# A ring of 24 weight places instead of 22, each on a 1 KB boundary, paid for with the descriptor scratch

## The chip, the core and the metric

The kernel runs on one core of a Trainium2 chip. The metric is the device time of one execution in microseconds. Before the change the median of three runs is 1161.49 us (1161.32 to 1161.6). Engine names are those of the profile: PE is the matrix engine, DVE the vector engine, ACT the scalar engine, POOL the GpSimd engine, SP the engine that here issues nearly all loads; PEld is PE's weight load.

## What is computed

One layer of an encoder on a sequence of 256 tokens of width 1024, all in float32: a mixer (the "trunk" below), a layer norm, a mixture of 32 experts of which each token uses 4, and a second layer norm. Cut to the part that takes most of the time:

```
x  = layer_norm(alpha * x + mix(x))             # attention, pooling and an S5 branch, gated
logits = x @ w_router + b_router                 # 32 experts, the 4 largest per token
hu  = x_e @ w_up[e] + b_up[e]                    # 1024 -> 2048, for the tokens of expert e
act = x_glu * sigmoid(1.702 * x_glu) * (x_lin + 1)   # both clamped at 7
y_e = act @ w_down[e] + b_down[e]                # 1024 -> 1024
x  = layer_norm(alpha * x + sum_e gate_e * y_e)
```

The weights of one expert are 12 MB (2048 x 1024 and 1024 x 1024 numbers of 4 bytes), those of all 32 are 384 MB. Every weight is read from HBM once.

## The kernel before

**The ring.** All large weights come in chunks of 1 MB: 128 partitions of 8 KB. The trunk has 29 chunks (`N_TRUNK`), the experts 384: the experts are worked off in 16 pairs, and a pair has 24 chunks, 16 for `w_up` and 8 for `w_down`, the two experts in turn. The chunks live in a ring of `NW` places of 8 KB per partition (`place`, L82). `load_more` (L105) issues a load on SP's queue whenever a place is free, in the order of use; `done` (L122) gives a place back when the last product that reads its chunk has been written into the program, and so triggers the next load. The load itself then waits, in SP's queue, until PE has really read the place. Only the last two chunks differ: they are loaded together, in quarters with rows of 2 KB (L112 to L117).

**Places that hold something else.** At the start (L160) 12 places are taken from the ring for the trunk's own tiles (the input split in two halves, tables, work tiles); 10 are left for chunks. The trunk's tiles give their places back at fixed points (L702 to L710, L742 to L745), others ask for one (`keep`, L195, which takes the next place to come free). Near the end, in the last pair (L1144 to L1147), five places are taken for `row`, `base`, `z2` and two `lns`: the last loads have been issued by then.

**One pair.** Each token row of an expert sits in one of 64 slots. `up_chunk` (L1033) adds the bias and runs 16 chunk products for a quarter of the up projection; PE handles the two experts of a pair side by side, in two halves of its columns. `swiglu` runs on DVE and ACT between the matmuls. `gather` (L958) makes the next pair's inputs. `down_chunk` (L1041) runs the down projection, and `scatter` adds the gated result to four accumulators that stay in PSUM over all 16 pairs. In the last pair `residual` (DVE) and `add_residual` (PE) add the residual, and after the last scatter the second layer norm runs on all engines and the result goes out in four stores.

**The small loads.** `down_bias` (L1051), after pair 8, loads the 128 KB of `b_down` on POOL's queue into the tile that held the gated activations, and multiplies it with the gates in the next pair. `row_loads` (L1067), emitted in the last pair after `up_chunk(15, 1)`, loads the four rows of the layer norms' gains and offsets (4 KB each) on POOL's queue into one place of the ring, and POOL spreads each over all partitions (L1071). ACT's next instruction in the program after that point is the tanh of `swiglu` for `hu` of (15, 0).

**Completion counters.** A load signals its landing through one of eight counters that the program builder hands out in turn to all loads on SP's and ACT's queues together; a load waits until the one before it on the same counter has landed. Loads on POOL's queue have counters of their own.

**The place in memory.** Of each partition's memory, the first 16384 bytes are the descriptor scratch for POOL's loads, then come 128 bytes of constants, then the tiles of the pool `con` (L127 to L145, 3904 bytes with each tile rounded up to 32), then the ring. So the ring starts at 20416, which is 64 bytes below a multiple of 1 KB, and since a place is 8 KB every place does.

Of the kernel before, what the change touches and what calls it, by code (L numbers as in the profile page):

```python
# [7 lines left out]
F32 = mybir.dt.float32  # L8
# [10 lines left out]
NE = 32  # L19
NP = NE // 2  # L20
SLOT = 64
NW = 22
WARM = 8
ALPHA = 2.0 ** 0.25
EPS = 1e-5
# [38 lines left out]
def hybrid_layer(ctx: ExitStack, tc: tile.TileContext, wt, wm, pa, pb, pc, xin, bu, lnp, b_down, out):  # L64
    nc = tc.nc
    pe, act, dve, pool, sp = nc.tensor, nc.scalar, nc.vector, nc.gpsimd, nc.sync
    TT, TS, STT = dve.tensor_tensor, dve.tensor_scalar, dve.scalar_tensor_tensor

    con = ctx.enter_context(tc.tile_pool(name="con", bufs=1))
# [8 lines left out]
    state = {"next": 0}  # L78
    free = list(range(NW))
    wants = []  # L80
# [61 lines left out]
    ones32 = con.tile([128, 32], F32)  # L142
    epst = con.tile([128, 2], F32)
    hpi = con.tile([128, 1], F32)
    junk = con.tile([128, 1], F32)  # L145


    ph1 = ExitStack()
# [866 lines left out]
    def scatter(gT, y, n, first=False):  # L1015
        for t in range(2):
            pe.matmul(accs[t][n], gT[:, t * 128:(t + 1) * 128], y, start=first, stop=True, skip_group_check=True)  # L1017
# [32 lines left out]

    def down_bias():  # L1051
        bdn = mw.tile([32, D], F32, tag="at", name="bdn")
        pool.dma_start(out=bdn, in_=b_down)
        gTall = mw.tile([32, S], F32, tag="s0", name="gTall")
        pt = ph.tile([32, S], F32, tag="g", name="ptg")
        for t in range(2):
            pe.transpose(pt[:, t * 128:(t + 1) * 128], gate[:, t], ident)
        act.activation(out=gTall, in_=pt, func=ACTF.Copy)
        for n in range(2):
            pending.append(lambda n=n: scatter(gTall, bdn[:, n * 512:(n + 1) * 512], n))  # L1060
# [5 lines left out]

    def row_loads():  # L1067
        for i in range(4):
            pool.dma_start(out=row[32 * i:32 * i + 1, 0], in_=lnp[0, i:i + 1])
        for i in range(4):  # L1070
            pool.partition_broadcast(lns[i // 2][:, i % 2], row[32 * i:32 * i + 1, 0])  # L1071

# [65 lines left out]
    for p in range(NP):  # L1138
# [3 lines left out]
        for n in range(4):  # L1142
            hu = up_chunk(p, n, xg)
            if (p, n) == (NP - 1, 1):  # L1144

                row, base, z2, *lns = (place(free.pop(0)).rearrange("p (t d) -> p t d", t=2) for _ in range(5))
                row_loads()  # L1147
            if prev is not None:
                swiglu(*prev)
            if n == 2:  # L1150
                gT = gates_T(oh, gate[:, :, 2 * p:2 * p + 2])
            if n == 3 and p + 1 < NP:
                oh = hot(val[:, :, ahead])
            prev = (hu, at, n)
# [17 lines left out]
        if p + 1 == NP:  # L1172
            scatter(gT, y, 1)
        else:
            pending.append(lambda gT=gT, y=y, p=p: scatter(gT, y, 1, p == 0))
            if p == NP // 2:
                down_bias()
            xg = nxt
# [165 lines left out]
```

## Time and profile before

| | |
|---|---|
| median of 3 runs | 1161.49 us |
| profiled execution, its own time | 1161.53 us |
| span of the profiled execution | 1159.8 us |
| PE busy | 1130.4 us (97%) |
| PEld busy | 527.4 us (45%) |
| DVE, ACT, POOL busy | 300.9, 184.7, 13.5 us |
| moved by DMA | 438.05 MB, mean 378 GB/s |
| mean granted clock of TensorE | 0.997 |

The profile's page gives the busy time of each engine, then the span in 40 equal slices with the engines' busy tenths, the share of the 16 DMA engines' time that was used and the GB/s moved, then the groups of instructions and the loads. An engine's busy time is read against what the other engines did in the same stretch: ends of matmuls are modelled, so a PE that is shown busy is not thereby a PE at its peak. Waits are listed as "engine, line, what it waited for: total, times, longest".

### The profile page before, as it was taken

The numbers are of one execution on the slowest core, as the hardware profiler recorded it, in microseconds if no ns is written. First come the engines' busy times: TensorE is split into PE (matmuls) and PEld (weight loads), VectorE is DVE, ScalarE is ACT, GpSimd is POOL, SyncE is SP. The second block draws the span as 40 slices with busy tenths as digits, with TensorE's granted clock in tenths as the row PEclk, the third lists the DMA queues.
The fourth block names the chain that finished last, engine by engine and source line by source line (L and its number), as shares of the span: only waits on it lengthen the run. The fifth ranks groups of instructions, "written<-read, shape, count | busy, mean of one in ns | idle before, by whom it ended". The sixth has DMA issues, their size and how long they took to land. (4 is left out here: it accounts for less than half of the span.)

```text
span 1159.8 us, 13362 instructions
## 1 busy us (share of the span) xinstructions
PE 1130.4 (97%) x5535; PEld 527.4 (45%) x5535; DVE 300.9 (26%) x710; ACT 184.7 (16%) x389; POOL 13.5 (1%) x19
## 2 busy tenths in 40 slices
PE   9999999999999999999999999999999999999996
PEld 6888986643434343434343433343434344334332
DVE  4798622430202111111212121111111111111042
ACT  4555410310101010101010101010101010101002
POOL 0000000000000000000000000000000000000100
PEclk9999999999999999999999999999999999999999
DMA  9733685699999999999999999999999999999992
GB/s 368 306 110 137 243 358 212 253 423 421 420 421 421 421 421 421 421 421 420 421 422 420 421 421 420 414 422 420 422 421 420 422 420 421 421 421 420 420 412 87
DMA packets 63169, 438.05 MB, mean 378 GB/s; under 512 B 7136, under 2 KB 7648, under 8 KB 10752
## 3 DMA queue, kind: packets, MB, share of 16 engines
q1 hardware_dynamic: 62064, 435.46, 91.2%
q10 hardware_dynamic: 864, 1.54, 0.4%
q8 instruction: 45, 0.74, 0.3%
q0 software_dynamic: 176, 0.15, 0.0%
q14 instruction: 20, 0.16, 0.0%
HBM read 436.07 MB, written 1.05 MB: 377 GB/s over the span
## 5 line engine op out<-in xcount | busy, mean ns | idle before, releaser
L1028 PE MATMUL hu<-w,xg 128*64 128x512 f32 x2048 | 480.9, 596 | 14.2 <-DMA w<-in_wm_dram 14.2
L1028 PEld LDWEIGHTS hu<-w,xg 128*64 128x64 f32 x2048 | 166.0, 137 | 316.0 <-issue 262.1
L1028 PE MATMUL py<-w,at 128*64 128x512 f32 x1024 | 231.5, 597 | 0.0
L1000 DVE TENSOR_SCALAR s<-hu 128x256 f32<-128x256 f32 x64 | 27.0, 422 | 581.6 <-PE hu L1028 581.6
L1028 PEld LDWEIGHTS py<-w,at 128*64 128x64 f32 x1024 | 70.5, 136 | 136.0 <-issue 129.6
L1011 ACT ACTIVATE at<-pta 128x256 f32<-128x256 f32 x64 | 24.5, 383 | 422.9 <-PE pta L1010 422.9
L1037 PE MATMUL hu<-bup,pc_sb 128*64 128x512 f32 x256 | 68.3, 605 | 0.0
L1017 PE MATMUL acc<-y,gT 128*128 128x512 f32 x128 | 63.5, 618 | 1.5 <-ACT y L1045 1.5
L248 PE MATMUL pm<-w,w 128*128 128x256 f32 x208 | 60.6, 291 | 0.8 <-ACT vsb L641 0.8
L965 PE MATMUL pg<-oh,x 128*128 128x128 f32 x512 | 59.9, 275 | 0.0
L249 PE MATMUL pm<-w,w 128*128 128x256 f32 x208 | 58.8, 283 | 0.0
L250 PE MATMUL pm<-w,w 128*128 128x256 f32 x208 | 58.8, 282 | 0.0
L965 PEld LDWEIGHTS pg<-oh,x 128*128 128x128 f32 x512 | 58.4, 192 | 0.1
L1001 ACT ACTIVATE hu<-s 128x256 f32<-128x256 f32 x64 | 24.6, 385 | 168.3 <-DVE s L1000 168.3
L1045 ACT ACTIVATE y<-py 128x512 f32<-128x512 f32 x32 | 19.1, 597 | 190.9 <-PE py L1028 190.9
L234 DVE TENSOR_TENSOR w<-w,w 128x1024 fp32r<-128x1024 f32 x30 | 36.5, 1219 | 19.3 <-ACT w L233 19.1
L248 PEld LDWEIGHTS pm<-w,w 128*128 128x128 f32 x208 | 39.7, 191 | 3.8 <-issue 1.7
L1017 PEld LDWEIGHTS acc<-y,gT 128*128 128x128 f32 x128 | 21.7, 189 | 42.9 <-issue 39.7
L249 PEld LDWEIGHTS pm<-w,w 128*128 128x128 f32 x208 | 39.8, 191 | 0.1
L250 PEld LDWEIGHTS pm<-w,w 128*128 128x128 f32 x208 | 39.8, 191 | 0.0
L233 ACT ACTIVATE w<-w 128x1024 fp32r<-128x1024 f32 x30 | 31.6, 1057 | 35.3 <-PE pm L250 25.1
L408 PE MATMUL pm<-w,w 128*128 128x256 f32 x160 | 36.1, 383 | 1.1 <-DMA w<-in_wt_dram 1.1
(320 smaller groups left out, 681.8 us busy)
## 6 DMA issues: line engine op xcount, KB each, us to landing
w<-in_wm_dram SPq DMA_DIRECT2D x382, 1024.0 KB, 19.8
w<-in_wt_dram SPq DMA_DIRECT2D x26, 1024.0 KB, 7.9
w<-in_wm_dram SPq DMA_DIRECT2D x8, 256.0 KB, 11.7
w<-in_wt_dram SPq DMA_DIRECT2D x4, 256.0 KB, 5.6
w<-in_wt_dram ACTq DMA_DIRECT2D x4, 256.0 KB, 5.9
w<-in_wt_dram SPq DMA_DIRECT2D x2, 512.0 KB, 5.0
w<-in_xin_dram SPq DMA_DIRECT2D x1, 1024.0 KB, 7.7
w<-in_pb_dram SPq DMA_DIRECT2D x1, 896.0 KB, 8.5
```

The lines of the kernel that those rows point to most:

```text
L233: act.activation(out=hi, in_=src, func=ACTF.Copy)
L234: TT(lo, src, hi.bitcast(F32), op=ALU.subtract)
L248: pe.matmul(out, whi, ahi, start=first, stop=False)
L249: pe.matmul(out, whi, alo, start=False, stop=False)
L250: pe.matmul(out, wlo, ahi, start=False, stop=last)
L408: pe.matmul(dst, w[:, k * 128:(k + 1) * 128], xt3[:, k], start=(k == 0), stop=(k == 7))
L965: pe.matmul(pg[:, b], x1[:, t, k * 128:(k + 1) * 128], oh[:, t], start=(t == 0), stop=(t == 1))
L1000: TS(xg, hu[:, 0:256], 7.0, None, op0=ALU.min)
L1001: act.activation(out=th, in_=xg, func=ACTF.Tanh, scale=0.851)
L1017: pe.matmul(accs[t][n], gT[:, t * 128:(t + 1) * 128], y, start=first, stop=True, skip_group_check=True)
L1028: pe.matmul(dst[64 * e:64 * e + 64], lhs[:, k, 64 * e:64 * e + 64], w[:, k % 4], start=first and k == 0, stop=(k == 7))
L1037: pe.matmul(hu[64 * e:64 * e + 64], ident[:, i:i + 1].to_broadcast([128, 64]), bup, start=True, stop=False)
```

## The change

`NW` goes from 22 to 24. The descriptor scratch shrinks from 16 KB to 1 KB. The tile `junk` becomes a column of a tile `scr` of 96 bytes. The ring then starts at 1024 + 128 + 3872 + 96 = 5120 bytes, a multiple of 1 KB, and so does every place. The trunk still takes 12 places, from the end of a longer list; 12 are left for its chunks instead of 10. The load of `b_down` and the four row loads move from POOL's queue to ACT's; the spreading of the rows stays on POOL.

```diff
-NW = 22
+NW = 24
...
-    junk = con.tile([128, 1], F32)
+
+    scr = con.tile([128, 24], F32)
+    junk = scr[:, 0:1]
...
         bdn = mw.tile([32, D], F32, tag="at", name="bdn")
-        pool.dma_start(out=bdn, in_=b_down)
+        act.dma_start(out=bdn, in_=b_down)
...
         for i in range(4):
-            pool.dma_start(out=row[32 * i:32 * i + 1, 0], in_=lnp[0, i:i + 1])
+            act.dma_start(out=row[32 * i:32 * i + 1, 0], in_=lnp[0, i:i + 1])
...
-    nc = _bacc.Bacc("TRN2", target_bir_lowering=False, num_devices=1)
+    nc = _bacc.Bacc("TRN2", target_bir_lowering=False, num_devices=1, dynamic_dma_scratch_size=1024)
```

## Rows read from the trace of the kernel before

**Rows 1.** The page, span in 40 slices: DMA busy tenths, GB/s.
```profile
DMA  9733685699999999999999999999999999999992
GB/s 368 306 110 137 243 358 212 253 423 421 420 421 421 421 421 421 421 421 420 421 422 420 421 421 420 414 422 420 422 421 420 422 420 421 421 421 420 420 412 87
```
**Rows 2.** Windows: engines' busy us (instructions), PEclk, DMA share, GB/s.
```profile
180.00:200.00 20.00, 20.00 (x73) 13.52 (x72) 6.82 (x16) 0.00 (x0) 0.00 (x0) 1.00 0.52 204
200.00:220.00 20.00, 19.67 (x159) 13.56 (x158) 10.91 (x39) 7.58 (x14) 1.54 (x2) 1.00 0.75 286
220.00:231.00 11.00, 11.00 (x67) 5.74 (x67) 2.63 (x10) 1.83 (x4) 0.00 (x0) 1.00 0.32 117
231.00:240.00 9.00, 9.00 (x44) 2.98 (x42) 2.13 (x6) 1.05 (x3) 0.00 (x0) 1.00 1.01 422
240.00:1125.00 885.00, 870.38 (x3972) 334.99 (x3968) 148.19 (x360) 90.02 (x215) 7.70 (x9) 1.00 1.01 421
```
**Rows 3.** Waits of SP's queue: two of 177 to 231 us, one of 240 to 1125.
```profile
SPq L109 <- PE mix L789: 25.1, 3, 9.9
SPq L109 <- PE hu L1028: 10.1, 1, 10.1
...
SPq L109 <- DMA w<-in_wm_dram: 662.0, 318, 3.6
```
**Rows 4.** Waits of PE: one of 0 to 230 us, two of 340 to 1150.
```profile
PE pm L408 <- DMA w<-in_wt_dram: 1.1, 4, 0.6
...
PE hu L1028 <- DMA w<-in_wm_dram: 14.2, 24, 1.3
PE acc L1017 <- DMA bdn<-in_b_down_dram: 0.4, 1, 0.4
```
**Rows 5.** Timeline of PE: first bias product of pairs 2, 7, 9, 15.
```profile
330.46 1.03 PE L1037 MATMUL hu<-bup,pc_sb 128*64 128x512 f32 x4
...
603.63 1.03 PE L1037 MATMUL hu<-bup,pc_sb 128*64 128x512 f32 x4
...
721.27 1.08 PE L1037 MATMUL hu<-bup,pc_sb 128*64 128x512 f32 x4
...
1081.09 1.03 PE L1037 MATMUL hu<-bup,pc_sb 128*64 128x512 f32 x4
```
**Rows 6.** Timeline of the end: start, us, instruction [idle before <- what ended it].
```profile
1116.92 3.65 PE L1028 MATMUL hu<-w,xg 128*64 128x512 f32 x14 [0.41 <-DMA w<-in_wm_dram]
...
1121.90 0.20 PEld L1028 LDWEIGHTS py<-w,at 128*64 128x64 f32 x4 [0.84 <-DMA w<-in_wm_dram]
...
1126.26 1.98 PE L1083 MATMUL acc<-w,pc_sb 128*128 128x512 f32 x4 [0.34 <-DVE w L1078]
1129.38 1.98 PE L1083 MATMUL acc<-w,pc_sb 128*128 128x512 f32 x4 [1.14 <-DVE w L1078]
...
1155.82 0.36 ACTq L1210 DMA_DIRECT2D out_dram<-w  x1
```
**Rows 7.** The page, DMA issues: KB each, median us from issue to landing.
```profile
w<-in_wm_dram SPq DMA_DIRECT2D x382, 1024.0 KB, 19.8
```
**Rows 8.** One window among the loads in quarters, rows of 2 KB.
```profile
1128.00:1129.00 1.00, 0.24 (x1) 0.00 (x0) 0.96 (x2) 0.00 (x0) 0.00 (x0) 1.00 1.00 393
```
**Rows 9.** Timeline of POOL, ACT, PE: the small loads and what stands beside them.
```profile
721.72 0.83 POOL L1053 DMA_DIRECT2D bdn<-in_b_down_dram  x1 [505.58 <-DMA w<-in_wm_dram]
...
1091.50 1.93 POOL L1069 DMA_DIRECT2D w<-in_lnp_dram  x4 [368.95 <-PE hu L1028]
1099.39 4.94 POOL L1071 PARTITION_BROADCAST w<-w  x4 [5.97 <-DMA w<-in_wm_dram]
...
1091.73 0.39 ACT L1001 ACTIVATE hu<-s 128x256 f32<-128x256 f32 x1 [9.74 <-DVE s L1000]
...
1100.76 0.44 PE L1010 MATMUL pta<-pc_sb,s 128*128 128x128 f32 x2
...
0.73 1.86 ACTq L170 DMA_DIRECT2D w<-in_wt_dram  x4
```

## The prediction, made before the change was run

> **What bounds the kernel now.** I read the slices of the page first, then windows cut where the slices change, then the waits of SP and PE, last the timeline at the end. PE is shown busy for 97% of the span, and that row would mislead. The slices show two regimes of the DMA engines [rows 1]: in the first 230 us they are at nine tenths only at the start and idle for long stretches after it, and from the ninth slice on they stand at nine tenths and 420 to 423 GB/s up to the last but one. The windows give the edge: full from 231 us on (share 1.01), and 421 GB/s from 240 to 1125 us [rows 2].
>
> Whether PE waits for these loads is seen from the distance between pairs. From pair 2 to pair 7 a pair takes (603.63 - 330.46) / 5 = 54.63 us, from pair 9 to pair 15 (1081.09 - 721.27) / 6 = 59.97 us [rows 5]. The work of a pair is the same. 24 chunks of 1.0486 MB at 421 GB/s take 59.8 us. So the later pairs run at the pace of the loads, and the earlier ones at PE's own, 9% faster, off the stock that the ring had gathered in the trunk. PE's listed idle time for loads, 14.2 us in 24 waits [rows 4], is only the part that the modelled ends leave. The last waits for a load are at 1116.92 and 1121.90 us [rows 6]; what follows waits for DVE (1126.26, 1129.38) and runs down to the last store at 1155.82 without a load in its way.
>
> What held the loads back before 231 us is in SP's queue: between 177 and 231 us it waited for PE to finish reading places, 25.1 us in three waits on the trunk's last products and 10.1 us on the first expert's [rows 3]. The ring was full and the DMA engines had nothing to do. From 240 us on SP waits 662.0 us for earlier landings: there are eight in flight (19.8 us from issue to landing [rows 7], one landing every 2.49 us).
>
> **The change, part by part.** *Two more places.* They are free at the start, when the list of places is handed out: two more trunk chunks are loaded at once, and from then on each release triggers the load two chunks further on than before. When PE starts on the experts, two more chunks are in. Room for them: between 180 and 231 us the DMA engines are idle for 20 x 0.48 + 20 x 0.25 + 11 x 0.68 = 22.1 us [rows 2], and more before [rows 1]; two chunks need 2 x 1.0486 MB / 421 GB/s = 4.98 us. From 231 us on the stream is unbroken either way, so every landing comes 4.98 us earlier, that for which PE waits at 1121.90 too. PE starts the experts at the same time and has 9% of speed in hand; with 5.0 us more stock, and 59.97 - 54.63 = 5.34 us of it used up in a pair, it begins to wait about one pair later and still waits in the last pairs. The tail behind 1121.90 keeps its length. Term: -4.98 us. The bounds: no more than this from two places, and 0 if the advance is lost (below).
>
> *The trunk.* The two extra loads stand behind the loads that are needed first, and take about 5.0 us of DMA time in the first 50 us, where it is busy. PE waited for trunk chunks 1.1 us in 230 us [rows 4], and no chunk is issued later than before in the order of use. I take 0; the upper end is 5.0 us, if PE had to wait that long, which would be passed on in full, since the loads of the experts wait for PE there.
>
> *Places on a boundary.* The trace has no row of a load into a place that starts on one, so this is bounded by what each row costs apart from its bytes. With the share at 1.00, rows of 2 KB move at 393 GB/s [rows 8], rows of 8 KB at 421 [rows 2]. Per DMA engine that is 83.4 ns and 311.3 ns a row, so 227.9 ns for 6144 bytes, and about 7.4 ns that do not depend on the size, 2.4% of an 8 KB row. If the start 64 bytes below the boundary were all of it, the stream of 883 us from 239 to 1122 us would lose 21 us. The other end lies below nothing by as much as the slowest full slice, 414 GB/s against 421 [rows 1], 1.7% or 15 us. I take 0, by the row nearest to it: 421 GB/s in every slice with rows that all start off the boundary, and a fixed part that any row would have.
>
> [...]
>
> *The small loads on ACT.* `bdn` takes POOL 0.83 us at 721.72, PE waited 0.4 us for it [rows 4, 9]. On ACT it stands behind the copy of `y` and ahead of the copy of the gates, and waits for the same products as that `y`; its issue costs some 0.47 us by ACT's own four loads at the start (1.86 us [rows 9]). PE runs at the pace of the loads there and makes it up in the next pair: 0, between -0.4 and +0.5 us. The four row loads took POOL 1.93 us at 1091.50, as soon as the place was read [rows 9]. On ACT they are 1.86 us ahead of the tanh of (15, 0), queued behind them with everything that ACT does for that pair. ACT sat idle for 9.74 us before that tanh; with 24 places `row` gets one that PE has read half an up projection earlier, so the issue falls into this gap. And even when late, the transposes that need the tanh start at 1100.76, 9 us on. POOL spreads the rows at 1099.39 for 4.94 us, and their first reader, `residual`, comes after 1120. Term: 0; without the cover 1.86 us.
>
> *The smaller scratch* holds descriptors of loads on POOL's queue, of which none are left: 0.
>
> The sum is made on the profiled execution: 1161.53 - 4.98 = 1156.55 us. That execution is 0.04 us over the median of the runs, so 1156.5 us. The four zeros may move it by 1 us: 1155.5 to 1157.5.
>
> **The rivals.** *Loads into aligned places are faster.* For it: the fixed 7.4 ns a row [rows 2, 8]. Against it: nothing says that this is the offset. PE has the speed to follow (54.63 against 59.97 us a pair). In full 1156.5 - 21 = 1135.5 us; with half, 1146.
>
> *The advance is lost:* the extra loads make the trunk late by as much as they gain, or the stock is not there at 231 us. For it: the DMA engines are full in the first slice. Against it: 1.1 us of waits in the trunk, 22.1 us of idle DMA before 231. Time 1161.5 us.
>
> *ACT's queue becomes the wait, slower than before.* The moved loads now share the eight counters with SP's stream, and a row load may have to wait for a landing of the stream, with the tanh of (15, 0) behind it. Each turn of waiting costs 2.49 us; four in a row, 10 us, still lie in the gap and the cover above. From 18 us on (9.74 + 9) PE stands, and from 18 + 5 = 23 us the kernel is slower than before. If the rows were handed counters of the last loads, ACT would stand until 1137 - 5 = 1132 us; the transposes would start at about 1134 and not at 1095.8, and the time would be some 1195 us. Against it: POOL's rows were issued at once, between loads of the stream; nothing in the program puts them behind the last ones.
>
> *Aligned places are slower* by the 1.7% above: 1171 us.
>
> **How the numbers follow.** Forecast 0.76; faster loads 0.10; advance lost 0.07; ACT's wait 0.05; slower loads 0.02. 0.2% is 2.3 us, about what a measurement of this kernel can tell from no change. Faster by more than that: 0.76 + 0.10 = 0.86; within it 0.07; slower 0.05 + 0.02 = 0.07. The range goes from 1147 (the smaller half of the faster loads) to 1159 us: it holds 0.76 and about 0.05 of the rivals. The forecast's own range is 1155.5 to 1157.5.
>
> **What would show it.** In the profile after, full DMA from the same 231 us at the same 421 GB/s; pairs of PE 54.6 us apart up to pair 7 and 59.9 from pair 9 or 10 on, pair 15 starting near 1076; the last wait for a load at about 1117. A rate above 425 GB/s is the first rival; PE waits for loads in the first 230 us the second; an idle stretch of PE in the last pair ended by ACT the third. I am wrong on the main step if the last pairs do not wait for loads, or if pair 15 starts where it did.

## The result: 17.6 us less, and only 5 of them from the two places

The changed kernel takes 1143.99 us (median of 4 runs, 1143.88 to 1144.09), the kernel before on the same chip 1161.55 us (4 runs, 1161.32 to 1162.25). The ratio is 0.9848, with a 95% interval from 0.9831 to 0.9865. The forecast was 1156.5 us; the time lies 12.5 us below it, between the two prices that the first rival gave for faster loads (1146 and 1135.5). The profiled execution has a span of 1142.0 us and a time of its own of 1143.99 us. Of the ten executions of e4 below one took 4417.05 us; it is left out of the ratio there.

### The profile after

The slices of the page, as [rows 1]: DMA busy tenths, GB/s moved.

```profile
DMA  9923596599999999999999999999999999999992
GB/s 370 388 96 133 236 360 250 221 415 427 427 427 426 426 426 426 426 427 427 427 427 426 427 426 426 421 427 426 427 427 426 428 426 427 426 426 426 412 425 97
```

The DMA engines are still full from the ninth slice on, and they still have idle time before it. Two things are new. The second slice moves 388 GB/s instead of 306, some 2.2 MB more: the two extra chunks (e1, with 24 places, has 385 there, e2, with 22, has 308). And the rate: 426 or 427 GB/s in nearly every full slice, where [rows 1] had 420 to 422 in nearly all. The windows put this beside [rows 2] (engines' busy us with instructions in brackets, granted clock, DMA share, GB/s):

```profile
180.00:200.00 20.00, 20.00 (x74) 13.50 (x73) 6.84 (x16) 0.00 (x0) 0.00 (x0) 1.00 0.54 200
200.00:220.00 20.00, 19.67 (x161) 13.66 (x160) 10.92 (x39) 7.58 (x14) 1.54 (x2) 1.00 0.77 290
220.00:231.00 11.00, 11.00 (x66) 5.66 (x66) 2.63 (x10) 1.83 (x4) 0.00 (x0) 1.00 0.32 128
240.00:1100.00 860.00, 853.59 (x3942) 322.13 (x3940) 144.51 (x354) 89.43 (x213) 4.94 (x4) 1.00 1.01 426
```

From 180 to 231 us the kernel is nearly unchanged: the ring is full, and 0.46 x 20 + 0.23 x 20 + 0.68 x 11 = 21.3 us of DMA time stay idle (22.1 before). The stream then starts at the same moment, runs at the same share of 1.01 and carries 426 GB/s instead of 421. Nothing is faster by doing less: 382 loads of 1 MB stand on the page as in [rows 7], and each now lands 19.6 us after its issue, not 19.8:

```profile
w<-in_wm_dram SPq DMA_DIRECT2D x382, 1024.0 KB, 19.6
```

PE's timeline at the first bias product of pairs 2, 7, 9, 12 and 15, as [rows 5] (start, us of one, instruction):

```profile
330.25 1.03 PE L1039 MATMUL hu<-bup,pc_sb 128*64 128x512 f32 x4
...
603.42 1.03 PE L1039 MATMUL hu<-bup,pc_sb 128*64 128x512 f32 x4
...
713.11 1.08 PE L1039 MATMUL hu<-bup,pc_sb 128*64 128x512 f32 x4
...
886.72 1.03 PE L1039 MATMUL hu<-bup,pc_sb 128*64 128x512 f32 x4
...
1064.74 1.03 PE L1039 MATMUL hu<-bup,pc_sb 128*64 128x512 f32 x4
```

Pairs 2 to 7 are 54.63 us apart, as before: that is PE's own pace, and it has not moved. From pair 9 to 12 a pair takes (886.72 - 713.11) / 3 = 57.9 us, a mixture, and from 12 to 15 (1064.74 - 886.72) / 3 = 59.3 us, which is the pace of the loads again (24 x 1.0486 MB at 426 GB/s are 59.1 us). PE therefore starts to wait later, and the waits agree (engine, line, what it waited for: us in total, times, longest). Against [rows 4], 14.2 us in 24 waits, the same stretch of 340 to 1150 us now has

```profile
PE hu L1030 <- DMA w<-in_wm_dram: 6.3, 15, 1.2
```

and the trunk, where [rows 4] had 1.1 us in four waits, has one:

```profile
PE pm L410 <- DMA w<-in_wt_dram: 0.2, 1, 0.2
```

At the end, in place of [rows 6]:

```profile
1099.73 3.65 PE L1030 MATMUL hu<-w,xg 128*64 128x512 f32 x14 [0.28 <-DMA w<-in_wm_dram]
...
1104.69 0.20 PEld L1030 LDWEIGHTS py<-w,at 128*64 128x64 f32 x4 [0.83 <-DMA w<-in_wm_dram]
...
1109.06 1.98 PE L1085 MATMUL acc<-w,pc_sb 128*128 128x512 f32 x4 [0.35 <-DVE w L1080]
1112.18 1.98 PE L1085 MATMUL acc<-w,pc_sb 128*128 128x512 f32 x4 [1.14 <-DVE w L1080]
...
1138.27 0.40 ACTq L1212 DMA_DIRECT2D out_dram<-w  x1
```

The last two waits for a load end 17.19 and 17.21 us earlier than in [rows 6]. From the last of them to the last store the two kernels take 33.92 and 33.58 us. So all but 0.3 us of the gain is in when the loads land, and not in the tail. The place to look is the stream of loads between 231 and 1105 us.

### The profile page after: what moved, and what is told of

Its sections match the earlier page's. It is cut to its first block, busy times and chain, and to the rows that moved or that the text cites. A ratio compares the mean times of both kernels' runs of the same rounds, so it can differ in the third digit from the quotient of the medians.

```text
span 1142.0 us, 13355 instructions
## 1 busy us (share of the span) xinstructions
PE 1122.2 (98%) x5535; PEld 518.0 (45%) x5535; DVE 300.7 (26%) x710; ACT 184.8 (16%) x389; POOL 10.8 (1%) x14
## 5 line engine op out<-in xcount | busy, mean ns | idle before, releaser
L1030 PE MATMUL hu<-w,xg 128*64 128x512 f32 x2048 | 471.6, 596 | 6.4 <-DMA w<-in_wm_dram 6.3
L1030 PEld LDWEIGHTS hu<-w,xg 128*64 128x64 f32 x2048 | 155.7, 137 | 309.6 <-issue 278.7
L250 PE MATMUL pm<-w,w 128*128 128x256 f32 x208 | 60.6, 292 | 0.8 <-ACT vsb L643 0.8
L251 PE MATMUL pm<-w,w 128*128 128x256 f32 x208 | 58.8, 283 | 0.0
L252 PE MATMUL pm<-w,w 128*128 128x256 f32 x208 | 58.8, 283 | 0.0
L971 ACT ACTIVATE xg<-pg,pc_sb 128x128 f32<-128x128 f32 x64 | 29.3, 458 | 48.1 <-DVE xg L973 48.1
## 6 DMA issues: line engine op xcount, KB each, us to landing
w<-in_wm_dram SPq DMA_DIRECT2D x382, 1024.0 KB, 19.6
```

The costliest lines, as they stand in the source:

```text
L250: pe.matmul(out, whi, ahi, start=first, stop=False)
L251: pe.matmul(out, whi, alo, start=False, stop=False)
L252: pe.matmul(out, wlo, ahi, start=False, stop=last)
L971: act.activation(out=xg[:, k], in_=pg[:, b], func=ACTF.Identity, scale=l1[:, k:k + 1], bias=l1[:, 8 + k:9 + k])
L1030: pe.matmul(dst[64 * e:64 * e + 64], lhs[:, k, 64 * e:64 * e + 64], w[:, k % 4], start=first and k == 0, stop=(k == 7))
```

## The experiments

Theory after the result: the two places give the 5 us of the forecast, and the boundary gives the rest, through the rate. Rivals: the smaller scratch or the moved loads do it; or the alignment that counts is not that of the places, but of the source; or it needs 24 places to show. For reading the edits: the width of `scr` decides where the ring starts. With 24 floats it starts at 5120, and every 8 floats more or less move it, and with it every place and each tile behind the ring, by 32 bytes. All ratios are to the kernel before, run beside it.

### The four corners: places and boundary, each alone

**e1: all of the change, but places 64 bytes below a boundary of 1 KB** (192 past one of 256 bytes).

```diff
-    scr = con.tile([128, 24], F32)
+    scr = con.tile([128, 8], F32)
```

> The changed kernel with one thing undone: scr is 32 bytes instead of 96, so the ring of 24 starts 64 bytes below a 1 KB boundary, as before the change. Theory A (the boundary sped the loads up): the full windows fall from 426 to 421 GB/s, a chunk lands every 2.49 us instead of 2.46, and the time is 1144.0 + 11.4 = 1155.4 us (1154 to 1157). Theory B (the smaller scratch, the loads off POOL's queue or the 24 places sped them up): the rate stays at 426 and the time at 1144.

Measured: 1156.58 us (1155.88 to 1157.0), ratio 0.9953 [0.9936, 0.997]. The 12.6 us are gone, with 24 places, 1 KB of scratch and the small loads on ACT all still there. Three rows of e1's timeline, PE's, answer to the marks that the prediction set:

```profile
1076.44 1.03 PE L1039 MATMUL hu<-bup,pc_sb 128*64 128x512 f32 x4
...
1112.19 3.65 PE L1030 MATMUL hu<-w,xg 128*64 128x512 f32 x14 [0.40 <-DMA w<-in_wm_dram]
...
1117.17 0.20 PEld L1030 LDWEIGHTS py<-w,at 128*64 128x64 f32 x4 [0.84 <-DMA w<-in_wm_dram]
```

Pair 15 was to start near 1076 and the last wait for a load to end at about 1117. That is this kernel, not the changed one. PE's own pace has not moved with the tiles behind the ring: from pair 2 to pair 7 e1 takes 273.16 us, the changed kernel 273.17. The rate of e1's loads in the stream (window 240 to 1080 us) is 420 GB/s, where before had 421 from 240 to 1125 us:

```profile
240.00:1080.00 840.00, 829.04 (x3819) 321.55 (x3817) 137.89 (x340) 87.78 (x209) 0.00 (x0) 1.00 1.01 420
```

**e2: the kernel before, 22 places, and only the places put on the boundary.** Its scratch stays at 16 KB and its small loads on POOL; the ring starts at 20480.

```diff
-    junk = con.tile([128, 1], F32)
+    scr = con.tile([128, 24], F32)
+    junk = scr[:, 0:1]
```

> The kernel before with one thing done: scr of 96 bytes in place of junk, so the ring of 22 starts on a 1 KB boundary (28 KB less 8 KB); 16 KB of scratch, small loads on POOL as before. Theory A: 426 GB/s and 1161.5 - 11.4 = 1150 us (1149 to 1152). Theory B: 421 GB/s and 1161.5 us.

Measured: 1149.16 us (1148.92 to 1149.4), ratio 0.989 [0.9874, 0.9907]. Two lines that move an address by 64 bytes are worth 12.6 us, and the rate goes with them:

```profile
240.00:1080.00 840.00, 833.09 (x3842) 314.67 (x3839) 137.88 (x341) 87.61 (x208) 1.00 (x2) 1.00 1.01 426
```

**e4: the rest alone.** 22 places off the boundary, with the small scratch and the small loads on ACT.

```diff
-NW = 24
+NW = 22
...
-    scr = con.tile([128, 24], F32)
+    scr = con.tile([128, 8], F32)
```

> The changed kernel with 22 places and the ring 64 bytes below a 1 KB boundary: what is left of the change is the 1 KB scratch and the small loads on ACT. Theory A: 421 GB/s, and the time of before plus what the small loads on ACT cost; SP's stream waits for their landing twice (8.5 us for b_down, up to 7.0 us for a row in the changed kernel), which left 1.3 us of DMA time unused there: 1161.5 to 1163 us. Theory B: 426 GB/s and about 1150 us.

Measured: 1161.42 us (median of 10 runs), ratio 0.9997 [0.9987, 1.0007]. The interval holds 1: the scratch and the moved loads together are worth nothing that can be measured.

With these, each part has a price on either side of the other (before is 1161.80 us in this set of runs; the changed kernel's 1143.99 us stand beside 1161.55):

| | 22 places | 24 places | two places are worth |
|---|---|---|---|
| 64 below the boundary | 1161.42 (e4) | 1156.58 (e1) | -4.84 us |
| on the boundary | 1149.16 (e2) | 1143.99 (after) | -5.17 us |
| the boundary is worth | -12.64 us (before to e2) | -12.59 us (e1 to after) | |

The two add up within 0.3 us, as is to be expected of terms that both bring forward the end of one unbroken stream. e2 has its small loads on POOL and 16 KB of scratch, which e4 prices at nothing; against e8 below, where they are on POOL too, two places are worth 4.20 us (1144.96 against 1149.16). That the boundary needs the 24 places has fallen.

### Which boundary, and what being off it costs

**e3: 256 bytes past the multiple of 1 KB.**

```diff
-    scr = con.tile([128, 24], F32)
+    scr = con.tile([128, 88], F32)
```

> The changed kernel with scr of 352 bytes: the ring of 24 starts 256 bytes past a 1 KB boundary. If a 256-byte boundary is all that a row needs: 426 GB/s, 1144 us. If it needs 512 bytes or 1 KB: about 421 GB/s, 1155 us. Theory B: 1144 us either way.

Measured: 1143.76 us (1143.5 to 1144.09), ratio 0.9845 [0.9829, 0.9861]. The whole gain is there, so 1 KB is not what matters: a start 256 bytes past it does as well.

```profile
240.00:1080.00 840.00, 834.09 (x3862) 314.84 (x3860) 140.10 (x343) 87.93 (x209) 3.87 (x4) 1.00 1.01 426
```

Four more starts, between two multiples of 256 bytes: **e5** (64 past), **e9** (128 past), **e6** (32 past), **e10** (224 past).

```diff
-    scr = con.tile([128, 24], F32)
+    scr = con.tile([128, 40], F32)   # e5;  e9: 56,  e6: 32,  e10: 16
```

> The changed kernel with scr of 160 bytes: every place starts 64 bytes past a 256-byte boundary (1144.0 us on it, 1156.6 us at 192 past it, 12.6 us apart). [...]

> The changed kernel with scr of 224 bytes: every place starts 128 bytes past a 256-byte boundary. [...] If a start on 128 bytes is enough: 1144.0 us. [...]

> The changed kernel with scr of 128 bytes: every place starts 32 bytes past a 256-byte boundary. [...]

> The changed kernel with scr of 64 bytes: every place starts 224 bytes past a 256-byte boundary, an odd multiple of 32 as the start at 32 past it, which gave 1159.1 us. If odd multiples of 32 cost a second step on top of the first: 1159.1 us. If the start at 32 was dear for another reason: 1156.7 us. [...]

| start past a multiple of 256 | us (lowest to highest) | ratio and interval |
|---|---|---|
| 0 (after; e3) | 1143.99; 1143.76 | 0.9848 [0.9831, 0.9865]; 0.9845 [0.9829, 0.9861] |
| 64 (e5) | 1156.78 (1156.25 to 1157.18) | 0.9958 [0.9944, 0.9972] |
| 128 (e9) | 1156.49 (1155.86 to 1156.59) | 0.9955 [0.9939, 0.9972] |
| 192 (e1) | 1156.58 (1155.88 to 1157.0) | 0.9953 [0.9936, 0.997] |
| 32 (e6) | 1159.13 (1158.62 to 1159.93) | 0.9979 [0.997, 0.9989] |
| 224 (e10) | 1159.5 (1158.92 to 1159.89) | 0.9982 [0.9972, 0.9991] |

There are three levels. Off the boundary by 64, 128 or 192 bytes the kernel takes 1156.5 to 1156.8 us, whatever the distance: one step of 12.6 us. At 32 and 224, odd multiples of 32, it takes 2.7 us more (1159.3 against 1156.6 in the mean). e6 showed this second step first (1159.13), and e10 came out at it (1159.5). Why there is one is not shown. The rates follow, in order e9, then e10:

```profile
240.00:1080.00 840.00, 829.35 (x3821) 321.82 (x3816) 137.98 (x340) 87.77 (x209) 0.00 (x0) 1.00 1.01 421
```

```profile
240.00:1080.00 840.00, 828.24 (x3806) 324.10 (x3803) 137.91 (x340) 87.68 (x210) 0.00 (x0) 1.00 1.01 419
```

A cost that grows with the bytes between the boundary and the start is excluded: it would set 32 lowest, and 64 and 192 apart.

**e7: places on the boundary, the source in HBM off it.** The array of expert weights gets 16 zero floats ahead of it, so that every row is read from 64 bytes further on; what is computed is the same.

```diff
+        if name == "wm":
+            a = np.concatenate([np.zeros(16, np.float32), a.reshape(-1)])
...
+            t = t[16:].rearrange("(e c p k) -> e c p k", e=32, c=12, p=128)
```

> The changed kernel with the experts' weights shifted by 64 bytes in HBM; the places stay on the boundary. If the cost of a start off the boundary lies on the writing side: 1144.0 us, 426 GB/s. [...]

Measured: 1144.79 us (1144.5 to 1145.94), ratio 0.9859 [0.9842, 0.9875]. No step: 0.8 us over the changed kernel, with intervals that overlap, where the same 64 bytes on the other side cost 12.8 (e5). From pair 2 to the last wait but one e7 takes 770.24 us, the changed kernel 769.48 and e5 781.62. The rate says it too:

```profile
240.00:1080.00 840.00, 834.24 (x3862) 314.46 (x3858) 140.47 (x344) 87.99 (x209) 2.65 (x3) 1.00 1.01 426
```

So the cost lies where the row is written, in the core's own memory: between the kernels of the tables above only the places moved, and moving the source does not bring the step. That reading from off a boundary costs nothing is not shown: where the array itself starts in HBM is not on record, and the stream need not show a cost on a side that doesn't set its pace.

**The size per row.** Between e1 and the changed kernel the last wait but one moves from 1112.19 to 1099.73, by 12.46 us. In e1 the stream ran some 881 us to that point (from 231), at about 421 GB/s 354 chunks; a chunk has 128 rows for 16 DMA engines, so each engine wrote 8 x 354 = 2830 rows: an estimate of 4.4 ns a row. (The rates, 311.3 ns a row at 421 and 307.7 at 426, give 3.6, with 0.7 of rounding.) The 7.4 ns of [rows 2, 8] are no measure for it, because the window of [rows 8] does not hold rows of 2 KB alone. Its packets:

```profile
DMA packets 131, 0.39 MB, mean 393 GB/s; under 512 B 17, under 2 KB 17, under 8 KB 105
```

The 131 - 105 = 26 packets that are left are rows of 8 KB, more than half of the bytes. In the changed kernel the window from 1114 to 1115 us is free of them, with 215 - 23 = 192 rows of 2 KB, all written on the boundary:

```profile
DMA packets 215, 0.39 MB, mean 393 GB/s; under 512 B 23, under 2 KB 23, under 8 KB 215
```

With its 393 GB/s and the 426 of the stream, the prediction's own working gives an aligned row 8.6 ns that don't depend on its size (an estimate from 1 us). So a fixed part of that size stays on the boundary, and the 4 ns of the offset come on top of it.

### The small loads and the dips of the stream

The changed kernel's stream has two dips, in slices 26 and 38 of the page, at the two points where the small loads now stand on ACT. Only the second is new: slice 26 has 414 GB/s before the change too, with `b_down` on POOL [rows 1]. Two windows at the second:

```profile
1060.00:1070.00 10.00, 10.00 (x42) 3.37 (x41) 0.00 (x0) 0.60 (x1) 0.00 (x0) 1.00 1.02 414
1070.00:1080.00 10.00, 9.85 (x41) 3.09 (x39) 2.67 (x4) 0.39 (x1) 3.40 (x3) 1.00 0.98 398
```

And SP's queue now waits for them, of which [rows 3] had nothing (first row over the whole span, second from 1050 to 1095 us):

```profile
SPq L109 <- DMA bdn<-in_b_down_dram: 8.5, 1, 8.5
```

```profile
SPq L109 <- DMA w<-in_lnp_dram: 2.5, 1, 2.5
```

The shared counters do bite, then, but the victim is SP and not ACT. (The 7.0 us that e4's expectation gives to a row are, in that view, a wait for a landing of the stream.) My theory was that this costs the stream 1.3 us. **e8** puts the small loads back on POOL and keeps all else.

```diff
-        act.dma_start(out=bdn, in_=b_down)
+        pool.dma_start(out=bdn, in_=b_down)
...
-            act.dma_start(out=row[32 * i:32 * i + 1, 0], in_=lnp[0, i:i + 1])
+            pool.dma_start(out=row[32 * i:32 * i + 1, 0], in_=lnp[0, i:i + 1])
```

> The changed kernel with one thing undone: b_down and the four rows are loaded on POOL's queue again, whose loads have counters of their own. Theory: in the changed kernel SP's stream stood twice behind the landing of a load on ACT's queue, and 10 us slices of 411, 413 and 398 GB/s instead of 426 are 1.3 us of lost transfer; without it the time is 1144.0 - 1.3 = 1142.7 us. Rival: the eight loads in flight cover the wait, the dips are the profiler's or code loads, and the time stays 1144.0 us.

Measured: 1144.96 us (1144.76 to 1145.6), ratio 0.9858 [0.9841, 0.9874]. The dip at the end is gone,

```profile
1060.00:1070.00 10.00, 10.00 (x43) 3.38 (x41) 0.00 (x0) 0.60 (x1) 0.00 (x0) 1.00 1.01 427
1070.00:1080.00 10.00, 10.00 (x41) 3.94 (x42) 1.70 (x4) 0.39 (x1) 3.38 (x6) 1.00 1.01 424
```

and neither of SP's two waits is left. The dip at `b_down` has stayed: 710 to 720 us move 411 GB/s in the changed kernel, 415 in e8. And the time is not shorter but 1.0 us longer, with intervals that overlap. The theory has fallen. e8's trace says where the difference is not (PE, pairs 2 and 15 and the last wait but one):

```profile
331.08 1.03 PE L1039 MATMUL hu<-bup,pc_sb 128*64 128x512 f32 x4
...
1065.53 1.03 PE L1039 MATMUL hu<-bup,pc_sb 128*64 128x512 f32 x4
...
1100.59 3.65 PE L1030 MATMUL hu<-w,xg 128*64 128x512 f32 x14 [0.28 <-DMA w<-in_wm_dram]
```

From pair 2 to pair 15 that is 734.45 us, in the changed kernel 734.49; to the last wait but one 769.51 and 769.48. So over the stretch that holds all the small loads the two take the same time, and what the second dip took from the stream did not reach PE. The 0.8 us stand ahead of pair 2 (331.08 against 330.25 us), before any of these loads; why that part took longer is not shown.

## Why the prediction was wrong

**The step that failed** is "Places on a boundary": "I take 0, by the row nearest to it: 421 GB/s in every slice with rows that all start off the boundary, and a fixed part that any row would have." Its term measured -12.6 us. The row chosen could not speak to the question: all its loads start 64 bytes below a boundary, so it shows what that alignment gives and nothing of the other. The steadiness of 421 GB/s over 30 slices was taken for a ceiling; it was the price of one alignment, paid by every row alike. Nor did [rows 2, 8] bear on it: the 7.4 ns come from a window that held rows of both sizes, and rows on the boundary have a fixed part of that size too (an estimate of 8.6 ns, above). On that count the step was right, "a fixed part that any row would have"; but it says nothing on what the offset adds. So the bound of 21 us had no ground, and that the 12.6 us lie inside it is luck. The range failed in the same place: it ended at 1147 us, though the prediction's own first rival reached down to 1135.5, since that rival was given a chance of 0.10.

**The offset in the runs.** It costs on the writing side (64 bytes in the places 1156.78 us, e5; 64 bytes in the source 1144.79, e7, with the reserve made there). A start 256 bytes past the multiple of 1 KB takes the time of one on it (e3, 1143.76, against 1143.99), and 192 bytes past a boundary cost what 64 do (e1 and e5, 1156.58 and 1156.78).

**Right, by the runs:**

- *Two more places*, -4.98 us: -4.84 and -5.17 (-4.20 against e8). The mechanism is the one described: two more chunks loaded in the first 57 us, idle DMA before 231 us, the same start of the unbroken stream, pair 15 and the last wait in e1 where they were put. PE had the speed to follow the other 12.6 us as well, since it runs at 54.63 us a pair and still waits in the last pairs.
- *The trunk*, 0: one wait of 0.2 us in the changed kernel, and pair 2 starts at 330.25 us, before at 330.46.
- *The small loads* and *the smaller scratch*, 0: e4's interval holds 1, and e8 takes the same time as the changed kernel from pair 2 to the last waits. The load of `b_down` and the four row loads stand on ACT as described, the rows in the gap ahead of the tanh:

```profile
713.01 0.34 ACTq L1055 DMA_DIRECT2D bdn<-in_b_down_dram  x1
...
1069.23 1.34 ACTq L1071 DMA_DIRECT2D w<-in_lnp_dram  x4
1075.21 0.39 ACT L1003 ACTIVATE hu<-s 128x256 f32<-128x256 f32 x1 [9.57 <-DVE s L1002]
```

**The rivals.** *Loads into aligned places are faster* is what happened, at more than its half and less than its whole, though the 7.4 ns it was priced by were misread; it had a chance of 0.10, too little for a mechanism that no row spoke against. Its condition, that PE can follow, was met. *The advance is lost* and *aligned places are slower* are excluded by e1 and e2. *ACT's queue becomes the wait* did not come: ACT issued the rows in 1.34 us and idled 9.57 us for DVE before the tanh.

## What to carry to other kernels

Where a kernel runs at the pace of its loads, look also at where in the core's memory the rows land: a start at a multiple of 256 bytes was worth 12.6 us of 1161 here, for 64 bytes, more than the two extra buffers that the change was named after. A steady rate is no proof of a ceiling if every transfer in the trace has the same start; only a run with another start can tell, and until then the range has to hold the rival's price. A rate is that of one size of row only if the packets of its window are all of that size, which the packet counts show. Extra places paid what the idle transfer time ahead of the stream could take in (here about 5.0 us for 2 MB), as long as the end waits for the stream.

## What the runs showed of the hardware that was not expected

- A row of 8 KB took each DMA engine some 4 ns longer (an estimate from e1 and the changed kernel) when it was written to a start off a multiple of 256 bytes, and the kernel took the same at 64, 128 and 192 bytes past it (1156.78, 1156.49, 1156.58 us against 1143.99); at 32 and 224 past, the stream lost another 2.7 us. Other distances were not tried; the gain stood with a start on a multiple of 1 KB and with one 256 bytes past it (1143.99 and 1143.76 us).
- Reading the rows from 64 bytes further on in HBM showed no such step (1144.79 against 1143.99 us).
- At full share, with one core of the chip at work, the stream of 8 KB rows ran at 426 GB/s over 840 us (e2, e3).
- The landing of a small load on ACT's queue held SP's queue for 8.5 us, a wait that is gone in e8, with the load on POOL; PE reached its last waits after the same time in both (769.48 and 769.51 us from pair 2).
